# Quarter sums of normed x2 and the weight rests in a fast-multiplied MLP: from GpSimd to VectorE, with copies out of PSUM

## The chip, the cores and the metric

The kernel runs on one core of a Trainium2 chip. The metric is the device time of an execution in microseconds, the median over runs. TensorE does the matrix products, ScalarE and VectorE do elementwise work and may read PSUM, GpSimd works on SBUF alone and also issues the transfers that add to what lies in SBUF, SyncE issues the plain transfers.

## The reference

One layer of a hybrid decoder: x is normed and projected, three token mixers run side by side, their merged output is projected and added to x. The sum is called x2 here. Then comes the part that the change touches:

```python
h2 = rms_norm(x, norm_ffn[l])                       # x is x2 in the kernel; 512 tokens x 1024 channels
up = causal_dwconv(h2 @ w_up[l], ffn_conv_w[l], ffn_conv_b[l])   # w_up: 1024 x 6144
gate_h, val_h = jnp.split(up, 2, axis=-1)
x = x + (jax.nn.gelu(gate_h, approximate=True) * val_h) @ w_down[l]
return rms_norm(x, final_norm)
```

All values are float32.

## The kernel before

**Split products.** TensorE multiplies in a format with fewer bits than float32. So every operand is split in two: `hi` is a copy by ScalarE into that format (line 97), `lo` is what is left, source minus `hi`, by VectorE (line 98, called the rest below). `mm3` (line 104) adds up three products, hi x hi, hi x lo, lo x hi; the products with a weight's `lo` come last. `split(hi, lo, src, eng)` puts the rest on another engine if one is given.

**Order of the work.** The program is a list of units (the matmuls of one weight piece) and steps. Each unit carries preparations that are emitted a given number of units ahead: `load` (a plain transfer by SyncE), `add` (a transfer by GpSimd that adds a second piece of the weights to what was loaded), `ready` (the split). The framework then orders each engine's instructions at build time by priority in program order and by its own estimate of when they are ready; each engine runs its list strictly in order. Tiles of SBUF that come from `fslot` and `rslot` share 51 slots of 128 x 512 float32, given out in the order of the program. `sbank` has three PSUM banks (`sm` in the trace), `bank` five (`mm`).

**Norm of x2.** While the last part of the output projection runs, each of four token tiles t is normed (`norm2`, with the reciprocal root as a chain of tiny VectorE steps, lines 112 to 118) and transposed by TensorE, four 128 x 128 blocks to a bank (`norm2_flip`, line 1147). Each bank is split into `h2["h"]` and `h2["l"]`, which hold all 1024 channels by 512 tokens. Tiles 2 and 3 are transposed among the first units of the up projection.

**The up projection** has 24 gate and 24 value tiles of 128 channels. Eighteen pairs go the ordinary way (`up_units`: 24 matmuls of 128 x 512 each). Six pairs (numbers 3, 4, 6, 7, 9, 10) go a fast way (`up_fast`): a 2 x 2 block product with seven products in place of eight. The blocks on the token side are the quarters A11, A12, A21, A22 of normed x2 (first index: half of the tokens, second: half of the channels). Their sums are S1 = A21 - A22, S2 = S1 - A11, A11 - A21 and A12 + S2. On the weights' side the sums B11 + B12 and so on are made by the adding transfers, in the one buffer B11: for a1 as loaded, then plus B12 for c1, plus B22 for b1, plus B21 for b3. The seven parts are named a1, a2, c1, c2, b1, b2, b3; each is 12 matmuls of 128 x 256.

`h2_sums(p)` (p is one of two halves of the channels within a quarter) makes the sums on GpSimd: four additions hi + lo to get the quarters back, four sums (lines 1212 to 1217). `h2_ready(key, p)` splits one sum. `up_fast` runs the rests of a2, c2 and b2 on GpSimd, those of a1, c1, b1, b3 on VectorE.

Around the first fast pair the order is: units 0 to 2, `h2_sums(0)`, unit 3, `h2_sums(1)`, units 4 and 5, `h2_ready` of all four sums for p = 0, a1, unit 6, `h2_ready` of all four for p = 1, c1, a2, c2. Its b1, b2 and b3 run among the parts of the next fast pair, which begins with b1 of the pair ahead and then its own a1.

After the up tiles the down projection follows, fast for the first 20 of 24 channel tiles, with adding transfers of its own on GpSimd (line 299).

Of the kernel before, what the change touches and what calls it, by code (L numbers as in the profile page):

```python
# [8 lines left out]
F32 = mybir.dt.float32  # L9
# [4 lines left out]
AF = mybir.ActivationFunctionType  # L14
ALU = mybir.AluOpType
# [3 lines left out]
P = 128  # L19
# [23 lines left out]
HT = S // 2  # L43
# [14 lines left out]
def trunk(ctx: ExitStack, tc: tile.TileContext, x, xT, mem, memT, par, wdecay, wch, wv, wg, wmk,  # L58
          wmv, wrg, wbr, wout, wup, wdown, wdown2, gffn, gfin, out):
    nc = tc.nc  # L60
# [11 lines left out]
    def nm(s):  # L72
        uid[0] += 1
        return f"{s}_{uid[0]}"

    def fslot(shape=(P, S)):
        return apool.tile(list(shape), F32, tag="s", name=nm("f"))

    def rslot(shape=(P, S)):
        return apool.tile(list(shape), F32R, tag="s", name=nm("r"))  # L80
# [14 lines left out]
    def split(hi, lo, src, eng=None):  # L95

        nc.scalar.activation(hi, src, AF.Copy)  # L97
        return (eng or nc.vector).tensor_tensor(out=lo, in0=src, in1=hi.bitcast(F32), op=ALU.subtract)  # L98
# [34 lines left out]
    def unit(dram, n, fn, parts=1):  # L133

        w = {}
        i = sum(1 for k, *_ in prog if k == "unit")

        def ready():
            w["w"] = fetch(dram, n, parts)
            for h in behind.get(i, ()):  # L140
                h()
        prog.append(("unit", [(AHEAD, ready)], lambda: fn(w["w"])))

    def made_unit(pre, fn):

        prog.append(("unit", pre, fn))

    def step(fn):
        prog.append(("step", [], fn))
# [194 lines left out]
    def run(*parts):  # L344

        for p in parts:
            if isinstance(p, tuple):
                unit(*p)
            else:
                for v in p:  # L350
                    made_unit(*v) if isinstance(v, tuple) else step(v)
# [37 lines left out]
    def x_norm(k):  # L389

        f = xs["h", k] = fslot()
        nc.vector.scalar_tensor_tensor(out=f, in0=xs["T"][k], scalar=col(C_GMIX + k), in1=xs["rb"],  # L392
                                       op0=ALU.mult, op1=ALU.mult)
        split(hh[:, k, :], hl[:, k, :], f)
# [49 lines left out]
    xn = [lambda k=k: x_norm(k) for k in range(KD)]  # L444
# [198 lines left out]
    def branch(n, acts, d, gt=None):  # L643

        g = [gt]

        def gate(ps):
            g[0] = fslot()
            nc.scalar.activation(g[0], ps, AF.Sigmoid)

        def proj(w):
            pp = channel_major(w, NM, lambda k: acts[k])
            if n == BRANCHES[0]:
                merged.append(mslot())
                nc.vector.tensor_tensor(out=merged[d], in0=pp, in1=g[0], op=ALU.mult)
                return
            nc.vector.tensor_tensor(out=g[0], in0=pp, in1=g[0], op=ALU.mult)
            nc.vector.tensor_tensor(out=merged[d], in0=merged[d], in1=g[0], op=ALU.add)
            if n == BRANCHES[2]:
                r = (rslot(), rslot())  # L660
                split(*r, merged[d])
                mr.append(r)
        return [proj_in(18 + 8 * n + d, gate), (wbr[n, d], MIX, proj)]
# [103 lines left out]
    b2 = [u for d in range(KD) for u in branch(2, oc, d)]  # L767
# [173 lines left out]
    at = lambda a, i: by_chunk(a)[:, :, i:i + 1].broadcast_to([DK, NT, P])  # L941
# [188 lines left out]
                                       op0=ALU.mult, op1=ALU.mult)  # L1130
        return xn

    h2 = {}

    def norm2(t):
        y = rstd(t)
# [2 lines left out]
    def norm2_flip(t):  # L1139
        if t == 0:  # L1140
            h2["h"] = hpool.tile([P, KD, S], F32R, name="h2h", tag="hh")
            h2["l"] = hpool.tile([P, KD, S], F32R, name="h2l", tag="hl")
        xn = h2.pop(("xn", t))
        for g in range(2):
            pt = sbank((P, 4, P))
            for k in range(4):
                nc.tensor.transpose(pt[:, k, :], xn[g][:, k * P:(k + 1) * P], ident)
            split(*(h2[a][:, 4 * g:4 * g + 4, t * P:(t + 1) * P] for a in "hl"), pt)

    step(lambda: gain_rows(gffn))  # L1150
    wo = down_units(wout, lambda k: mr[k], norm2, norm2_flip)
# [52 lines left out]
    h2s = {}  # L1204

    def h2_sums(p):
        tt, f = nc.gpsimd.tensor_tensor, {}
        for r in range(2):
            for c in range(2):
                at = slice(4 * c + 2 * p, 4 * c + 2 * p + 2), slice(r * HT, (r + 1) * HT)  # L1210
                f[r, c] = fslot((P, 2, HT))
                tt(out=f[r, c], in0=h2["h"][(slice(None), *at)].bitcast(F32), in1=h2["l"][(slice(None), *at)].bitcast(F32),
                   op=ALU.add)
        tt(out=f[1, 1], in0=f[1, 0], in1=f[1, 1], op=ALU.subtract)
        tt(out=f[1, 0], in0=f[0, 0], in1=f[1, 0], op=ALU.subtract)
        tt(out=f[0, 0], in0=f[1, 1], in1=f[0, 0], op=ALU.subtract)
        tt(out=f[0, 1], in0=f[0, 1], in1=f[0, 0], op=ALU.add)
        h2s.update({("c1", p): f[1, 1], ("b2", p): f[1, 0], ("b1", p): f[0, 0], ("c2", p): f[0, 1]})

    def h2_ready(key, p):  # L1220
        f, h2s[key, p] = h2s[key, p], (rslot((P, 2, HT)), rslot((P, 2, HT)))
        split(*h2s[key, p], f)

# [6 lines left out]
    def up_fast(i, keep):  # L1230

        src = lambda q: wup[NF * (int(q[2]) - 1) + i][:, HB * (int(q[1]) - 1):HB * int(q[1])]
        raw, w, st = {}, {}, {}

        def load(q):
            raw[q] = fslot()
            loads.append(nc.sync.dma_start(raw[q], src(q)))

        def ready(key, q, more=None):
            w[key] = rslot(), rslot()  # L1240
            split(*w[key], raw[q], nc.gpsimd if key in ("a2", "c2", "b2") else None)
            if more:
                add(q, more)

        def add(q, more):
            nc.gpsimd.dma_start(raw[q], src(more), accum_op=ALU.add)

        def run(key):
            if key == "a1":
                st["x"], st["o"] = bank((P, HT)), (fslot(), fslot())  # L1250
            elif key in ("a2", "c1"):
                st[key] = sbank((P, HT))
            ps = st["c1" if key[0] == "c" else "a2" if key == "a2" else "x"]
            hi, lo = w.pop(key)
            k = range(KD // 2)
            mm3(ps, [(*(a[:, j * P:(j + 1) * P] for a in (hi, lo)), *h2_part(key, j)) for j in k],
                key in ("a1", "a2", "c1"), True, key not in ("a1", "a2", "c1"))
            (g, v), tt = st["o"], nc.vector.tensor_tensor

            one, two = slice(0, HT), slice(HT, S)  # L1260
            if key in ("a1", "c1", "c2", "b3"):
                o = {"a1": g[:, one], "c1": v[:, two], "c2": v[:, one], "b3": g[:, two]}[key]
                nc.scalar.activation(o, ps, AF.Copy)
            elif key == "a2":
                tt(out=g[:, one], in0=g[:, one], in1=ps, op=ALU.add)
            else:
                o = v[:, one if key == "b1" else two]
                tt(out=o, in0=o, in1=ps, op=ALU.subtract)
            if key == "b3":
                up_mix(*(up_evac(a, NF * half + i) for half, a in enumerate((g, v))), i, keep)  # L1270

        pre = {
            "a1": [(8, lambda: load("B11")), (3, lambda: ready("a1", "B11", "B12"))],
            "a2": [(6, lambda: load("B21")), (3, lambda: ready("a2", "B21"))],
            "c1": [(2, lambda: ready("c1", "B11", "B22"))],
            "c2": [(6, lambda: load("B22")), (3, lambda: ready("c2", "B22"))],
            "b1": [(2, lambda: ready("b1", "B11", "B21"))],
            "b2": [(9, lambda: load("B12")), (6, lambda: add("B12", "B22")), (3, lambda: ready("b2", "B12"))],
            "b3": [(2, lambda: ready("b3", "B11"))],
        }  # L1280
        return {key: (p, lambda key=key: run(key)) for key, p in pre.items()}
# [110 lines left out]
    def halves(i, a):  # L1392
# [2 lines left out]

    group = lambda first: lambda k: acts[first + k]
    us = up_units((0, 1, 2, 5, 8, 11), whole, 3)
    run(*us[:3], [lambda: h2_sums(0)], us[3], [lambda: h2_sums(1)], us[4], us[5],
        [lambda k=k: h2_ready(k, 0) for k in ("c1", "c2", "b1", "b2")])

    ahead = None
    for i, u in zip((3, 4, 6, 7, 9, 10), us[6:]):
        f = up_fast(i, whole)
        run([ahead["b1"]] if ahead else [], [f["a1"]], u)
        if not ahead:
            run([lambda k=k: h2_ready(k, 1) for k in ("c1", "c2", "b1", "b2")])
        run([ahead["b2"]] if ahead else [], [f["c1"], f["a2"]], [ahead["b3"]] if ahead else [], [f["c2"]])
        ahead = f
    us = up_units(range(12, 20), whole)
    run([ahead["b1"]], us[0], [ahead["b2"]], us[1], [ahead["b3"]])  # L1410
# [97 lines left out]
```

## Time and profile before

| | before |
|---|---|
| median of 3 runs | 935.45 us (934.63 to 937.51) |
| profiled execution | 935.83 us |
| its span, first to last instruction | 934.1 us |
| TensorE busy | 916.4 us (98%) |
| VectorE, ScalarE, GpSimd busy | 660.1, 518.3, 174.3 us |

The profile is of one execution. Times in it count from the start of the span. A row of a timeline gives start, duration, engine, line, operation, the tiles out<-in and the number merged into the row; in brackets stands the idle time ahead and what ended it. PE is TensorE's matmul, PEld its weight load, DVE VectorE, ACT ScalarE, POOL GpSimd, SP SyncE. A row of a group gives busy time and mean nanoseconds of one. The granted clock is the share of full speed that TensorE was given. In the trace, `r` is any split tile from `rslot`, `f` any tile from `fslot`, `wlo`/`whi` the split of an ordinary weight, `h2h`/`h2l` the split of normed x2.

### The profile page before, as it was taken

Reading aid. Unit: us, or ns where it says so; the run is one execution under the profiler, and the core shown is the slowest. Engines: PE = TensorE matmul, PEld = TensorE weight load, DVE = VectorE, ACT = ScalarE, POOL = GpSimd, SP = SyncE. Lnnn points to the kernel's source line nnn. Section 1 sums busy time; section 2 is a strip of 40 time slices with the busy share of each in tenths; the row PEclk is TensorE's granted clock in tenths of the full one; section 3 lists DMA queues with packets and bytes.
Section 4 is the critical chain, followed back from the end, with each engine's and each line's share of the span. In section 5 each row is a group of like instructions: output and inputs, shape, how many; then the busy total and the mean of one; then the engine's idle time right before and its main releaser. Section 6 shows DMA issues by size and latency. Waiting matters only on the chain.

```text
span 934.1 us, 12758 instructions
## 1 busy us (share of the span) xinstructions
PE 916.4 (98%) x4606; PEld 785.9 (84%) x4606; DVE 660.1 (71%) x1142; ACT 518.3 (55%) x872; POOL 174.3 (19%) x202
## 2 busy tenths in 40 slices
PE   9999999999999999999999999899999999999997
PEld 7898888888889998888888897899977888888885
DVE  6997754665788666847676758666787766688865
ACT  7675655684865577484434335455555445544544
POOL 0010000000233430330000136445410231013102
PEclk9999999999999999999999999899999999999999
DMA  7446223223369873321167214675645676356622
GB/s 255 135 136 207 95 78 100 87 74 117 99 145 207 188 196 107 116 77 46 57 184 254 69 35 125 150 177 128 144 113 158 135 210 150 95 136 183 150 68 90
DMA packets 51184, 123.28 MB, mean 132 GB/s; under 512 B 6145, under 2 KB 14001, under 8 KB 51121
## 3 DMA queue, kind: packets, MB, share of 16 engines
q1 hardware_dynamic: 35648, 94.99, 31.0%
q0 software_dynamic: 15328, 27.21, 16.9%
q8 instruction: 36, 0.59, 0.3%
q14 instruction: 28, 0.22, 0.1%
q10 hardware_dynamic: 144, 0.26, 0.1%
HBM read 117.99 MB, written 3.67 MB: 130 GB/s over the span
## 4 chain that ended last, share of the span: by engine, by line
PE 79%; DVE 9%; DMA 5%; issue 3%; ACT 2%; POOL 0%; SPq 0%; POOLq 0%; ACTq 0%; DVEq 0%
PE mm L104 71%; DMA f<-in_wup 3%; PE sm L104 3%; DVE wlo L98 2%; PE mm L436 2%; DVE r L98 2%; DMA raw<-in_wup 2%; DVE f L1164 1%; DMA f<-in_wdown 1%; ACT r L97 1%; ACT whi L97 0%; DVE f L1129 0%; PE sm L211 0%; DVE f L392 0%; PE sm L996 0%
## 5 line engine op out<-in xcount | busy, mean ns | idle before, releaser
L98 DVE TENSOR_TENSOR wlo<-raw,whi 128x1024 fp32r<-128x1024 f32 (+3 forms) x142 | 163.6, 1156 | 86.7 <-ACT whi L97 42.6
L97 ACT ACTIVATE whi<-raw 128x1024 fp32r<-128x1024 f32 (+3 forms) x142 | 135.6, 960 | 138.7 <-PE mm L104 107.4
L104 PE MATMUL mm<-whi,r 128*128 128x512 f32 (+2 forms) x568 | 171.9, 373 | 1.9 <-DVE r L98 1.9
L104 PEld LDWEIGHTS mm<-whi,r 128*128 128x128 f32 x568 | 105.4, 188 | 19.1 <-DVE r L98 3.5
L104 PE MATMUL mm<-hh,whi 128*128 128x512 f32 x288 | 113.3, 394 | 0.0
L104 PE MATMUL mm<-hl,whi 128*128 128x512 f32 x288 | 112.7, 391 | 0.0
L104 PE MATMUL mm<-wlo,r 128*128 128x512 f32 (+2 forms) x284 | 105.7, 372 | 0.5 <-DVE wlo L98 0.5
L104 PE MATMUL mm<-h2l,whi 128*128 128x512 f32 x264 | 102.8, 390 | 0.0
L104 PE MATMUL mm<-h2h,whi 128*128 128x512 f32 x264 | 102.7, 390 | 0.0
L104 PE MATMUL mm<-r,whi 128*128 128x512 f32 (+1 forms) x432 | 94.2, 367 | 0.0
L98 DVE TENSOR_TENSOR wlo<-f,whi 128x512 fp32r<-128x512 f32 (+2 forms) x90 | 53.7, 631 | 49.9 <-ACT whi L97 43.8
L98 DVE TENSOR_TENSOR r<-f,r 128x512 fp32r<-128x512 f32 (+3 forms) x126 | 73.0, 601 | 20.4 <-ACT r L97 20.0
L97 ACT ACTIVATE r<-f 128x512 fp32r<-128x512 f32 (+3 forms) x144 | 70.1, 534 | 30.1 <-DMA f<-in_wup 25.5
L104 PEld LDWEIGHTS mm<-r,whi 128*128 128x128 f32 x432 | 75.2, 189 | 13.1
L97 ACT ACTIVATE whi<-f 128x512 fp32r<-128x512 f32 (+2 forms) x90 | 48.1, 579 | 65.1 <-PE mm L104 47.3
L104 PE MATMUL mm<-hh,wlo 128*128 128x512 f32 x288 | 71.5, 390 | 0.0
L104 PE MATMUL mm<-r,r 128*128 128x512 f32 (+2 forms) x336 | 65.5, 346 | 0.0
L299 POOL DMA_DIRECT2D f<-in_wdown x40 | 35.1, 1041 | 162.2 <-DVE wlo L98 117.0
L104 PE MATMUL mm<-h2h,wlo 128*128 128x512 f32 x264 | 65.2, 389 | 0.0
L104 PEld LDWEIGHTS mm<-hh,wlo 128*128 128x128 f32 x288 | 54.0, 188 | 11.2
L104 PEld LDWEIGHTS mm<-hh,whi 128*128 128x128 f32 x288 | 54.1, 188 | 10.8
L104 PEld LDWEIGHTS mm<-hl,whi 128*128 128x128 f32 x288 | 54.1, 188 | 10.7
(262 smaller groups left out, 1613.1 us busy)
## 6 DMA issues: line engine op xcount, KB each, us to landing
raw<-in_wch SPq DMA_DIRECT2D x39, 512.0 KB, 3.4
raw<-in_wup SPq DMA_DIRECT2D x36, 512.0 KB, 4.0
f<-in_wdown POOLq DMA_DIRECT2D x40, 256.0 KB, 7.6
raw<-in_wbr SPq DMA_DIRECT2D x24, 384.0 KB, 3.1
raw<-in_wdown SPq DMA_DIRECT2D x14, 512.0 KB, 4.1
f<-in_wup SPq DMA_DIRECT2D x24, 256.0 KB, 6.8
f<-in_wup POOLq DMA_DIRECT2D x24, 256.0 KB, 5.7
f<-in_wdown SPq DMA_DIRECT2D x20, 256.0 KB, 5.7
```

The source lines that it names most:

```text
L97: nc.scalar.activation(hi, src, AF.Copy)
L98: return (eng or nc.vector).tensor_tensor(out=lo, in0=src, in1=hi.bitcast(F32), op=ALU.subtract)
L104: nc.tensor.matmul(ps, lhsT=l, rhs=r, start=first and i == 0, stop=last and i == len(seq) - 1, skip_group_check=more)
L299: nc.gpsimd.dma_start(raw[to, p][j], src(q, p)[:, j, :], accum_op=ALU.add)
L436: nc.tensor.matmul(ps[u], lhsT=w(a, u, k), rhs=xs["r"][k][j], start=k == 0 and i < n, stop=k == KD - 1 and i >= len(seq) - n)
L1164: nc.vector.scalar_tensor_tensor(out=a[:, j:], in0=ps[:, :S - j], scalar=col(C_FCW + 48 * (2 - j) + f), in1=a[:, j:], op0=ALU.mult, op1=AL ...
```

## The change

Five edits:

- `norm2_flip` copies each transposed bank out of PSUM by ScalarE, in two pieces of 128 x 256, into eight tiles that hold the quarters of normed x2 unsplit.
- `h2_sums` takes these quarters and makes three sums a half, on VectorE and in place; the fourth (A11 - A21) is made by `h2_sum3` when it is split.
- In `up_fast` the rests of a2, c2 and b2 go to VectorE.
- `h2_ready` moves: c1 for both halves ahead of unit 5, c2 behind unit 5, b1 and b2 behind c2 of the first fast pair.
- No arithmetic is left on GpSimd in the up projection; its adding transfers stay.

```diff
@@ norm2_flip
-        xn = h2.pop(("xn", t))
+        xn, pts = h2.pop(("xn", t)), []
         for g in range(2):
             pt = sbank((P, 4, P))
             for k in range(4):
                 nc.tensor.transpose(pt[:, k, :], xn[g][:, k * P:(k + 1) * P], ident)
             split(*(h2[a][:, 4 * g:4 * g + 4, t * P:(t + 1) * P] for a in "hl"), pt)
+            pts.append(pt)
+
+        for g, pt in enumerate(pts):
+            for p in range(2):
+                if t % 2 == 0:
+                    h2f[t // 2, g, p] = fslot((P, 2, HT))
+                nc.scalar.activation(h2f[t // 2, g, p][:, :, t % 2 * P:(t % 2 + 1) * P], pt[:, 2 * p:2 * p + 2, :], AF.Copy)
@@ h2_sums
-        tt, f = nc.gpsimd.tensor_tensor, {}
-        for r in range(2):
-            for c in range(2):
-                at = slice(4 * c + 2 * p, 4 * c + 2 * p + 2), slice(r * HT, (r + 1) * HT)
-                f[r, c] = fslot((P, 2, HT))
-                tt(out=f[r, c], in0=h2["h"][(slice(None), *at)].bitcast(F32), in1=h2["l"][(slice(None), *at)].bitcast(F32),
-                   op=ALU.add)
-        tt(out=f[1, 1], in0=f[1, 0], in1=f[1, 1], op=ALU.subtract)
-        tt(out=f[1, 0], in0=f[0, 0], in1=f[1, 0], op=ALU.subtract)
-        tt(out=f[0, 0], in0=f[1, 1], in1=f[0, 0], op=ALU.subtract)
-        tt(out=f[0, 1], in0=f[0, 1], in1=f[0, 0], op=ALU.add)
-        h2s.update({("c1", p): f[1, 1], ("b2", p): f[1, 0], ("b1", p): f[0, 0], ("c2", p): f[0, 1]})
+        sub, add = ALU.subtract, ALU.add
+        a11, a12, a21, a22 = (h2f.pop((r, c, p)) for r in range(2) for c in range(2))
+        s2 = fslot((P, 2, HT))
+        tt = nc.vector.tensor_tensor
+        tt(out=a22, in0=a21, in1=a22, op=sub)
+        tt(out=s2, in0=a22, in1=a11, op=sub)
+        tt(out=a12, in0=a12, in1=s2, op=add)
+        h2s.update({("c1", p): a22, ("c2", p): a12, ("b1", p): s2, ("b2", p): (a11, a21)})
+
+    def h2_sum3(p):
+        a11, a21 = h2s["b2", p]
+        nc.vector.tensor_tensor(out=a11, in0=a11, in1=a21, op=ALU.subtract)
+        h2s["b2", p] = a11
 
     def h2_ready(key, p):
+        if key == "b2":
+            h2_sum3(p)
         f, h2s[key, p] = h2s[key, p], (rslot((P, 2, HT)), rslot((P, 2, HT)))
         split(*h2s[key, p], f)
@@ up_fast, ready
-            split(*w[key], raw[q], nc.gpsimd if key in ("a2", "c2", "b2") else None)
+            split(*w[key], raw[q])
@@ the order around the first fast pair
-    run(*us[:3], [lambda: h2_sums(0)], us[3], [lambda: h2_sums(1)], us[4], us[5],
-        [lambda k=k: h2_ready(k, 0) for k in ("c1", "c2", "b1", "b2")])
+    run(*us[:3], [lambda: h2_sums(0)], us[3], [lambda: h2_sums(1)], us[4], [lambda: h2_ready("c1", 0), lambda: h2_ready("c1", 1)],
+        us[5], [lambda: h2_ready("c2", 0), lambda: h2_ready("c2", 1)])
...
         run([ahead["b1"]] if ahead else [], [f["a1"]], u)
+        run([ahead["b2"]] if ahead else [], [f["c1"], f["a2"]], [ahead["b3"]] if ahead else [], [f["c2"]])
         if not ahead:
-            run([lambda k=k: h2_ready(k, 1) for k in ("c1", "c2", "b1", "b2")])
-        run([ahead["b2"]] if ahead else [], [f["c1"], f["a2"]], [ahead["b3"]] if ahead else [], [f["c2"]])
+            run([lambda k=k, p=p: h2_ready(k, p) for k in ("b1", "b2") for p in range(2)])
```

2 lines of the change are left out of this document (1 added, 1 removed).

## The prediction

> **What bounds the kernel now.** I read the page's head, then TensorE's waits, then the stretches of the MLP (window table), then the timelines of the stretch that stands out. The head says how little there is to win: TensorE is busy in all but 17.7 us of the span, so a change to other engines can give back only its gaps and what a gap costs afterwards.
>
> ```profile
> span 934.1 us, 12758 instructions
> PE 916.4 (98%) x4606; PEld 785.9 (84%) x4606; DVE 660.1 (71%) x1142; ACT 518.3 (55%) x872; POOL 174.3 (19%) x202
> ```
>
> Two lines of TensorE's waits in the window 500 to 720 (what waits, for what: us in total, times, longest) and two of the window table (PE, PEld, DVE, ACT, POOL busy, then the granted clock):
>
> ```profile
> PE mm L104 <- DVE r L98: 3.2, 8, 1.0
> PE sm L104 <- POOL r L98: 2.7, 1, 2.7
> ...
> 580.20:586.30 6.10, 2.68 (x18) 2.19 (x17) 6.10 (x8) 4.44 (x8) 2.93 (x3) 1.00 0.35 93
> 586.30:593.10 6.80, 5.41 (x25) 4.97 (x24) 5.09 (x8) 3.47 (x7) 2.36 (x4) 0.50 0.69 245
> ```
>
> One hole carries most of it: from 580.2 to 586.3 TensorE works 2.68 of 6.10 us, and in the 6.8 us behind it the granted clock is 0.50. That is where the first fast tile runs its parts c1, a2, c2, b1:
>
> ```profile
> 580.21 0.73 PE L104 MATMUL sm<-r,r 128*128 128x256 f32 x4
> 581.68 0.39 PE L104 MATMUL sm<-h2h,r 128*128 128x256 f32 x1 [0.73 <-ACT r L97]
> ...
> 585.57 0.74 PE L104 MATMUL sm<-h2h,r 128*128 128x256 f32 x4 [2.69 <-POOL r L98]
> ...
> 587.36 1.86 PE L104 MATMUL sm<-r,r 128*128 128x256 f32 x7 [0.92 <-DVE r L98]
> 589.69 2.93 PE L104 MATMUL sm<-r,r 128*128 128x256 f32 x12 [0.47 <-ACT f L1263]
> ...
> 594.17 0.28 PE L104 MATMUL mm<-h2h,r 128*128 128x256 f32 x1
> ...
> 633.59 1.60 PE L104 MATMUL sm<-r,r 128*128 128x256 f32 x12
> 635.03 0.28 PE L104 MATMUL sm<-h2h,r 128*128 128x256 f32 x1
> ```
>
> A part of 12 matmuls takes 635.03 - 633.59 = 1.44 us when nothing waits, four take 5.8. Here they take 594.17 - 580.21 = 13.96. The hole costs 8.2 us: four waits of 0.73, 2.69, 0.92 and 0.47 (4.8 together), and some 3.4 from half speed (half of 6.8).
>
> Why it is there: GpSimd sums normed x2's quarters just ahead of it, and VectorE stands still meanwhile.
>
> ```profile
> 562.05 5.33 POOL L1212 TENSOR_TENSOR f<-h2h,h2l 128x512 f32<-128x512 f32 x4
> ...
> 562.84 5.64 DVE L98 TENSOR_TENSOR wlo<-raw,whi 128x1024 fp32r<-128x1024 f32 x1 [1.72 <-ACT whi L97]
> 569.95 1.59 DVE L1177 TENSOR_TENSOR f<-f,f 128x512 f32<-128x512 f32 x1
> 571.47 2.30 DVE L98 TENSOR_TENSOR wlo<-raw,whi 128x1024 fp32r<-128x1024 f32 x1
> 576.92 1.23 DVE L98 TENSOR_TENSOR wlo<-raw,whi 128x1024 fp32r<-128x1024 f32 x1 [1.71 <-ACT whi L97]
> 584.79 2.52 DVE L98 TENSOR_TENSOR r<-f,r 128x512 fp32r<-128x512 f32 x1
> ```
>
> The same 128x1024 rest takes 1.23 us with GpSimd quiet, 5.64 and 2.30 under its sums. With 0.68 for a 128x512 one (next fence), the excess is 4.41 + 0.91 + 1.07 + 1.84 = 8.2 us, on a queue that has one idle piece (1.71) from 562.84 until past 589.
>
> **The change part by part.** Rows that price it: two groups of GpSimd over the run, three of VectorE in the window 545 to 711, one of ScalarE.
>
> ```profile
> L98 POOL TENSOR_TENSOR r<-f,r 128x512 fp32r<-128x512 f32 x18 | 26.5, 1482 | 29.3 <-ACT r L97 27.6 <-DMA f<-in_wup 1.1 <-DVE f L1164 0.6
> L1212 POOL TENSOR_TENSOR f<-h2h,h2l 128x512 f32<-128x512 f32 x8 | 10.4, 1446 | 129.5 <-DVE st L116 117.2 <-DVE h2l L98 12.3
> ...
> L98 DVE TENSOR_TENSOR r<-f,r 128x512 fp32r<-128x512 f32 x32 | 26.2, 838 | 18.6 <-ACT r L97 18.5
> L98 DVE TENSOR_TENSOR wlo<-raw,whi 128x1024 fp32r<-128x1024 f32 x12 | 20.8, 1737 | 8.9 <-ACT whi L97 4.9 <-PE mm L104 4.0
> L98 DVE TENSOR_TENSOR h2l<-sm,h2h 128x512 fp32r<-128x512 f32 x3 | 2.0, 684 | 1.9 <-ACT h2h L97 1.9
> ...
> L1263 ACT ACTIVATE f<-sm 128x256 f32<-128x256 f32 x12 | 4.4, 370 | 3.4 <-PE sm L104 3.4
> ```
>
> *VectorE's bill.* It gets 18 rests (three for each of six fast tiles) and 8 quarter sums (six in h2_sums, two in h2_sum3), 26 x 0.684 = 17.8 us. It gets back what GpSimd took: 32 x (0.838 - 0.684) = 4.9 on rests and 12 x (1.737 - 1.23) = 6.1 on weight rests, 11 at least. So its busy time grows by about 7 us over 165, nothing where it idles; what counts is the place. GpSimd's 18 rests and 16 sums go to nothing.
>
> *Copies on ScalarE.* Sixteen of 128x256 from PSUM, 16 x 0.37 = 5.9 us, twelve of them in a stretch where ScalarE is busy 6.84 of 27 us, the last four behind the transposes at 546.86, where only the sums wait for them.
>
> ```profile
> 520.00:547.00 27.00, 26.23 (x162) 23.23 (x161) 21.43 (x72) 6.84 (x16) 2.55 (x2) 1.00 0.09 26
> ...
> 544.94 0.68 DVE L98 TENSOR_TENSOR h2l<-sm,h2h 128x512 fp32r<-128x512 f32 x1
> ...
> 546.86 1.04 PE L1147 MATMUL sm<-ident,f 128*128 128x128 f32 x8
> ```
>
> A copy reads the bank that VectorE's rest reads. If it must wait for that rest, the last copies of token tile 2 run from 545.6 to 546.4, and the transposes of tile 3, which want the bank, begin at 546.86: hidden by 0.4 us. Below zero is excluded; above, two copies late would cost 0.7. I take 0. What is queued behind a waiting copy on ScalarE is only the next tile's high parts, 1.5 us away in the same rows. [...]
>
> *Ahead of the hole.* GpSimd's first two sums stretch two of VectorE's one-column reciprocal-root steps, 0.16 us each when undisturbed, to 0.81 and 1.22: 1.7 us in the chain that ends in the rests TensorE waits for at 545.
>
> ```profile
> 534.04 2.55 POOL L1212 TENSOR_TENSOR f<-h2h,h2l 128x512 f32<-128x512 f32 x2 [117.23 <-DVE st L116]
> ...
> 534.54 0.81 DVE L117 TENSOR_TENSOR st<-st,st 128x1 f32<-128x1 f32 x1
> 535.39 1.22 DVE L118 SCALAR_TENSOR_TENSOR st<-st,st 128x1 f32<-128x1 f32 x1
> 536.64 0.16 DVE L116 TENSOR_TENSOR st<-st 128x1 f32<-128x1 f32 x1
> ...
> 545.08 0.74 PE L104 MATMUL mm<-h2h,r 128*128 128x256 f32 x4 [0.31 <-DVE r L98]
> ...
> 546.28 0.74 PE L104 MATMUL mm<-h2h,r 128*128 128x256 f32 x4 [0.46 <-DVE r L98]
> ```
>
> Both waits are shorter than 1.7, so -0.8 (bounds: 0, should the order change, and -0.8).
>
> *The hole itself.* VectorE had split c1's weights at about 583.1, just before the transfer in the next fence could be issued. From 562.84 to there are 20.2 us; less 1.71 idle and the first three excesses (4.41, 0.91, 1.07) that is 12.1 us of unstretched work. Afterwards it has three to six quarter sums more (2.1 to 4.1), the two rests of c1's second half now ahead of c1's weights (1.4), less the two of b1 and b2 now behind (1.4). That ends c1's weight rest near 578 to 579 instead of 583, before TensorE wants it (580.2, its last four matmuls 1 us later). a2's rest follows at +0.7, c2's at +1.4 or with a weight rest between at +2.5, against needs of 582.6 and 584. So c1, a2 and c2 run without a wait: end 580.2 + 4.3 = 584.5. Next late is b1. Its weights are B11 plus a transfer that GpSimd may issue only when c1's split has read B11:
>
> ```profile
> 583.37 0.86 POOL L1246 DMA_DIRECT2D f<-in_wup  x1 [7.62 <-DVE r L98]
> ...
> f<-in_wup POOLq DMA_DIRECT2D x24, 256.0 KB, 5.7
> ```
>
> Issued near 578.5, landed at 584.2 to 585, split on ScalarE and VectorE by 586; and b1's own quarter sums are split behind it, because slots are given out in program order and h2_ready("b1") now stands after c2. Four more splits in a row, 0.6 each: b1 ends near 588.2 and the next a1 near 589.6, not at 587.4. I take 2.2 us lost here (bounds 0.5 and 3.6, by the landing). Gain 8.2 - 2.2 = 6.0, if the clock stays up.
>
> *The later fast tiles.* b3's rest is late by a quarter us in two tiles, because GpSimd does a rest before it issues the transfer that b3 reads:
>
> ```profile
> 637.92 0.74 PE L104 MATMUL mm<-h2h,r 128*128 128x256 f32 x4 [0.25 <-DVE r L98]
> ...
> 632.35 0.69 DVE L98 TENSOR_TENSOR r<-f,r 128x512 fp32r<-128x512 f32 x1 [3.81 <-ACT r L97]
> ...
> 634.21 1.77 POOL L1246 DMA_DIRECT2D f<-in_wup  x2
> ```
>
> VectorE ended at 633.04, the issue came at 634.21. With no rest on GpSimd it comes 1.1 us sooner: -0.5 for both. VectorE's three extra rests a tile (2.05) lie in its idle pieces, such as the 3.81. If that cover were gone, the whole 2.05 would show, six times 2.05 = 12.3.
>
> *Not touched.* Of the 3.2 us, what is left (about 1.9) are four waits from 694 to 708 for the down projection's activations. Nothing of the change stands in their chain, so I leave them.
>
> Sum: -6.0 - 0.8 - 0.5 = -7.3 on a profiled execution of 935.83 us (span 934.1 and 1.7 around it). That execution lies 0.4 above the median of 935.45, so I forecast 928.1 for the median.
>
> **The rivals.** *The clock falls again.* It fell with 3.4 us of idle time inside 6.1. If b1's wait comes to about that, half speed costs up to 3.4 once more: near 931.5. For it: the wait I expect (2.2) is of that kind. Against: it is a third less, and comes behind full work. [...]
>
> *The change doesn't do what it says.* Up to c1's split VectorE is given six sums (4.1) and two rests (1.4) for the 8.2 it gets back. If GpSimd's sums are only half of what stretches it (transfers write to SBUF at the same time), 4.1 comes back for 5.5 and the hole stays: 934 to 937. Against: the 5.64 begins and ends with the 5.33 of GpSimd's row, and the next rest but one, with transfers running, takes 1.23.
>
> *Slower: VectorE sets the pace of the fast tiles.* The mechanism is one: c1's weights are split only 0.55 us before TensorE takes them (633.04 against 633.59), and need to be complete 0.96 later. A rest put into VectorE's queue ahead of that one, and itself waiting for a transfer, holds it. From 1.5 us of delay a tile TensorE pays. To eat 7.3 us it must pay 1.2 us in each of six tiles; were all 2.05 us paid, 928.1 + 12.3 = 940.4.
>
> **How the numbers follow.** Likeliest as summed, 0.50: 925.6 (nothing lost at b1: 935.45 - 9.5 = 925.9, rounded down) to 930. Below that, with part of the 1.9 gone as well, 0.05. Clock falls again, 0.22: 930 to 933. No gain, 0.13: 933 to 938. Slower, 0.10: 938 to 941. A difference below 0.3% (2.8 us) is about what a measurement of this kernel can't tell from no change: faster means below 932.6, slower above 938.3. Faster 0.50 + 0.05 + 0.21 = 0.76, within 0.14, slower 0.10. The range leaves out the slow case and the two tails: 924.5 to 935.5.
>
> **What would show it.** Right: no GpSimd rows but transfers from 520 to 680; VectorE's 128x1024 rests at 1.23 throughout; c1, a2 and c2 in the first fast tile in 4.3 us with clock 1.00; a short wait at b1 with ScalarE held by a transfer. Wrong at its root: VectorE rests still stretched with GpSimd quiet; the same 2.69 under another releaser; or waits for VectorE's r of more than 1 us in every fast tile.

## The result and the profile after

| | before | after |
|---|---|---|
| median of 4 runs | 935.88 us | 923.61 us (922.28 to 924.37) |
| ratio, 95% interval | 1 | 0.9866 (0.9846 to 0.9886) |
| the same kernels again, with the experiments | 935.98 us | 924.64 us, ratio 0.9873 (0.9855 to 0.9892) |
| profiled execution, its span | 935.83, 934.1 us | 924.37, 922.6 us |

The kernel is about 12 us faster, 3.5 to 4.5 more than by the forecast of 928.1, and its first median lies just under the range (924.5 to 935.5). The page's head and, from it, TensorE's waits between 500 and 720 us after the change:

```profile
span 922.6 us, 12732 instructions
PE 912.0 (99%) x4606; PEld 784.1 (85%) x4606; DVE 657.2 (71%) x1168; ACT 524.1 (57%) x888; POOL 128.1 (14%) x168
```

```profile
PE mm L104 <- DVE f L1278: 0.7, 1, 0.7
PE mm L104 <- ACT r L97: 0.3, 1, 0.3
PE mm L104 <- ACT h2h L97: 0.2, 1, 0.2
```

None of the eight waits for VectorE's `r` (3.2 us) and not the one for GpSimd's (2.7) is left in this profile; one new wait is there, 0.68 us for VectorE to read a PSUM bank. (A second profile of the same kernel, a_again below, has two waits for VectorE's `r` again, 0.8 us together, and not the new one.) TensorE's row of the window from unit 6 to unit 7, where the hole was (PE, PEld, DVE, ACT, POOL busy, granted clock, DMA share, GB/s), and its timeline there:

```profile
577.27:590.57 13.30, 13.04 (x85) 11.81 (x84) 9.13 (x15) 7.16 (x13) 2.58 (x3) 1.00 0.75 191
```

```profile
577.27 1.98 PE L104 MATMUL mm<-h2h,wlo 128*128 128x512 f32 x8
579.09 1.60 PE L104 MATMUL sm<-r,r 128*128 128x256 f32 x12
...
581.96 1.60 PE L104 MATMUL sm<-r,r 128*128 128x256 f32 x12
...
584.05 0.39 PE L104 MATMUL mm<-r,r 128*128 128x256 f32 x1 [0.26 <-ACT r L97]
...
585.84 1.00 PE L104 MATMUL mm<-r,r 128*128 128x256 f32 x7
586.68 0.40 PE L104 MATMUL mm<-h2h,r 128*128 128x256 f32 x2
```

c1, a2 and c2 follow each other without a pause from 579.09 to 583.40. Then the matmuls of b1 (`r,r`) and of the next a1 (`h2h,r`) alternate, and one wait of 0.26 is all that is left. VectorE just ahead of it, with no arithmetic on GpSimd:

```profile
570.07 0.68 DVE L98 TENSOR_TENSOR r<-f,r 128x512 fp32r<-128x512 f32 x1
572.44 1.23 DVE L98 TENSOR_TENSOR wlo<-raw,whi 128x1024 fp32r<-128x1024 f32 x1 [1.70 <-ACT whi L97]
```

**Where the time came from.** I cut the region into three stages at TensorE's first matmuls with a weight's rest (`h2h,wlo`) of one unit: from the first transpose of normed x2 to unit 6; from unit 6 to unit 7 (the hole); from unit 7 to a unit in the middle of the down projection's first stretch. The two last bounds in the kernel before and the kernel after:

```profile
578.32 0.84 PE L104 MATMUL mm<-h2h,wlo 128*128 128x512 f32 x3
599.27 1.07 PE L104 MATMUL mm<-h2h,wlo 128*128 128x512 f32 x4
...
713.02 1.30 PE L104 MATMUL mm<-h2h,wlo 128*128 128x512 f32 x5
```

```profile
577.27 1.07 PE L104 MATMUL mm<-h2h,wlo 128*128 128x512 f32 x4
590.57 0.61 PE L104 MATMUL mm<-h2h,wlo 128*128 128x512 f32 x2
...
701.43 0.84 PE L104 MATMUL mm<-h2h,wlo 128*128 128x512 f32 x3
```

All kernels in one table, each stage from one profile (both profiles where there are two), in us. Each ratio is to the kernel before as timed together with that kernel (its medians there are 935.88 to 936.84), so kernels are better compared by ratio than by median:

| kernel | to unit 6 | the hole | unit 7 to 713 | sum | median | ratio (95%) |
|---|---|---|---|---|---|---|
| before | 53.55, 53.41 | 20.95, 20.46 | 113.75, 114.30 | 188.2 | 936 | 1 |
| after | 52.39, 52.26 | 13.30, 13.20 | 110.86, 111.62 | 176.8 | 923.61, 924.64 | 0.9866, 0.9873 |
| b_rests | 53.61 | 20.89 | 109.13 | 183.6 | 932.96 | 0.9966 (0.9955 to 0.9978) |
| b_order | 53.22 | 18.68 | 113.03 | 184.9 | 935.05 | 0.9984 (0.9970 to 0.9999) |
| a_oldorder | 52.56 | 18.90 | 109.12 | 180.6 | 928.50 | 0.9914 (0.9899 to 0.9930) |
| a_gprests | 52.57 | 14.18 | 114.54 | 181.3 | 928.73 | 0.9923 (0.9908 to 0.9939) |
| a_dummy | 54.13 | 19.43 | 109.27 | 182.8 | 930.93 | 0.9940 (0.9925 to 0.9954) |
| a_b12early | 52.58 | 13.67 | 112.40 | 178.7 | 926.12 | 0.9887 (0.9867 to 0.9906) |
| a_nocopies | 52.26 | 16.70 | 111.35 | 180.3 | 928.42 | 0.9908 (0.9890 to 0.9926) |
| a_lastb2 | 52.27 | 13.40 | 110.83 | 176.5 | 925.39 | 0.9879 (0.9859 to 0.9899) |
| a_zrests | 52.26 | 14.73 | 114.71 | 181.7 | 931.10 | 0.9943 (0.9929 to 0.9956) |
| a_b1first | 52.28 | 14.24 | 109.13 | 175.7 | 925.26 | 0.9880 (0.9863 to 0.9897) |
| b_load7 | 54.16 | 21.37 | 112.12 | 187.7 | 937.23 | 1.0009 (0.9996 to 1.0022) |
| a_load7 | 52.57 | 13.15 | 109.71 | 175.4 | 924.27 | 0.9878 (0.9855 to 0.9901) |
| b_lastb2 | 53.96 | 21.31 | 112.29 | 187.6 | 935.27 | 0.9993 (0.9980 to 1.0006) |

So the change gave 1.2 us up to unit 6, 7.5 in the hole and 2.8 behind it, together 11.4 of the 11.3 to 12.3 by the medians. Among kernels that do the same there, the first two columns spread by up to 0.9 us. The third spreads by 1.5 where GpSimd makes all 18 rests (113.0 to 114.5 in before, b_order and a_gprests) and by 3.3 where it makes none (109.1 to 112.4 in the kernel after, b_rests, a_oldorder, a_dummy, a_b12early, a_nocopies and a_b1first). The two groups don't overlap, but differences within a group are not read from one profile. The expectations split the third column once more, at the low-part matmuls of 690.91 (682.36 after): "later fast tiles" are 91.64 us before and 91.79 after, the "first down-projection stage" 22.11 and 19.07.

### The profile page after: what moved, and what is told of

It reads as the page before. It is cut to its first block, busy times and chain, and to the rows that moved or that the text cites. A ratio compares the mean times of both kernels' runs of the same rounds, so it can differ in the third digit from the quotient of the medians.

```text
span 922.6 us, 12732 instructions
## 1 busy us (share of the span) xinstructions
PE 912.0 (99%) x4606; PEld 784.1 (85%) x4606; DVE 657.2 (71%) x1168; ACT 524.1 (57%) x888; POOL 128.1 (14%) x168
## 4 chain that ended last, share of the span: by engine, by line
PE 87%; DMA 5%; DVE 3%; issue 2%; ACT 2%; POOL 0%; SPq 0%; DVEq 0%; POOLq 0%; ACTq 0%
PE mm L104 78%; DMA f<-in_wup 4%; PE sm L104 3%; DMA f<-in_wv 2%; PE mm L436 2%; DVE wlo L98 1%; DVE r L98 1%; ACT r L97 1%; PE sm L211 0%; PE sm L996 0%; PE sm L983 0%; PE sm L1010 0%; DVE f L810 0%; PE sm L1147 0%; PE sm L601 0%
## 5 line engine op out<-in xcount | busy, mean ns | idle before, releaser
L98 DVE TENSOR_TENSOR wlo<-raw,whi 128x1024 fp32r<-128x1024 f32 (+3 forms) x142 | 157.4, 1113 | 82.8 <-ACT whi L97 39.4
L98 DVE TENSOR_TENSOR r<-f,r 128x512 fp32r<-128x512 f32 (+3 forms) x144 | 79.7, 577 | 23.0 <-ACT r L97 22.7
L104 PEld LDWEIGHTS mm<-r,r 128*128 128x128 f32 (+1 forms) x336 | 53.3, 186 | 9.6 <-ACT r L97 0.5
```

Source lines behind the costliest of these rows:

```text
L104: nc.tensor.matmul(ps, lhsT=l, rhs=r, start=first and i == 0, stop=last and i == len(seq) - 1, skip_group_check=more)
```

## The experiments

**The rests alone.** b_rests: the line of `ready` as in the kernel after, all else as before.

```diff
-            split(*w[key], raw[q], nc.gpsimd if key in ("a2", "c2", "b2") else None)
+            split(*w[key], raw[q])
```

> The kernel before, with one part of the change alone: the rests of the weight sums of a2, c2 and b2 on VectorE; the sums of the quarters stay on GpSimd and the order of their splits is the old one. Theory A (GpSimd's sums stretch VectorE and so make the hole): the 128x1024 rests of 5.6 and 2.3 us stay, c1, a2, c2 and b1 of the first fast tile still need 12 to 15 us, b3's small waits go (-0.5), and the time is 935 down to 932, the lower end if GpSimd's last rest was also what made the down projection 3 us late. Theory C (a2's rest on GpSimd is the cause, the 2.69 us wait): the hole shrinks by that wait and by the half clock behind it, some 6 us, to 928 to 930.

932.96 us, so 3.2 us gained by the ratio, none of it in the hole (20.89): there the rest that TensorE waits for is merely made by another engine. The 2.69 us for GpSimd's `r` turn into waits for VectorE's:

```profile
585.44 0.73 PE L104 MATMUL sm<-h2h,r 128*128 128x256 f32 x4 [1.97 <-DVE r L98]
586.01 0.28 PE L104 MATMUL sm<-r,r 128*128 128x256 f32 x1
587.95 1.86 PE L104 MATMUL sm<-r,r 128*128 128x256 f32 x7 [1.66 <-DVE r L98]
```

Theory C falls. The gain is all behind unit 7: 109.13 for 114, which is 4.9 us in a profile that ran 1.2 us under this kernel's median. The change as a whole shows only 2.8 there. The three kernels with no rests on GpSimd but a hole of 18.9 us or more (b_rests, a_oldorder, a_dummy) have 109.1 to 109.3, so part of what the closed hole saves may be waited for again behind it; a_b1first has 109.13 with the hole closed, so this is not shown.

**The rests back.** a_gprests: the kernel after with that line as before.

> The kernel after, with the rests of a2, c2 and b2 back on GpSimd; the sums stay on VectorE from ScalarE's copies, in the new order. Theory A: the hole stays closed (c1 and a2 without a wait over 1 us); b3's quarter-us waits come back. If the 3.0 us of the first down-projection stage hang on the rest on GpSimd ahead of it, they are lost too: 926 to 927.5; if they hang on something else, 924 to 925. Theory C: a wait for GpSimd's rest of 2 us or more in the first fast tile and 929 or more.

928.73 us. The hole stays closed (14.18), no wait for GpSimd's `r` comes back, and the third column is as long as before (114.54). That is theory A, but with 1.2 us more than its upper end; the 0.5 us that I gave for the rests can no longer be right.

**The old order.** a_oldorder: the kernel after, `h2_ready` called where it was.

```diff
-    us[4], [lambda: h2_ready("c1", 0), lambda: h2_ready("c1", 1)],
-        us[5], [lambda: h2_ready("c2", 0), lambda: h2_ready("c2", 1)])
+    us[4], us[5],
+        [lambda k=k: h2_ready(k, 0) for k in ("c1", "c2", "b1", "b2")])
...
+            run([lambda k=k: h2_ready(k, 1) for k in ("c1", "c2", "b1", "b2")])
```

> The kernel after, with the order of the quarters' splits put back (all four of the first half behind the sixth unit, all four of the second ahead of c1); sums and rests stay on VectorE. Theory A: VectorE has four rests (2.7 us) more ahead of c1's weights, which were ready about 1.7 us early: a wait of 0.5 to 2 us at c1 or a2, clock 1.00, 924 to 927. Theory B (the order is what fills the hole): most of 7.6 us comes back, 929 to 932.

928.50. No arithmetic on GpSimd, and the hole is there all the same: 18.90.

```profile
582.27 0.74 PE L104 MATMUL sm<-h2h,r 128*128 128x256 f32 x4 [0.55 <-DVE r L98]
...
584.79 1.60 PE L104 MATMUL sm<-r,r 128*128 128x256 f32 x7 [1.66 <-DVE r L98]
586.96 2.93 PE L104 MATMUL sm<-r,r 128*128 128x256 f32 x12 [0.57 <-ACT f L1273]
```

```profile
585.20:592.00 6.80, 6.22 (x29) 5.93 (x29) 3.98 (x7) 3.36 (x7) 1.75 (x2) 0.50 0.70 197
```

Each wait is as short as I expected (0.55, 1.66, 0.57), but I had written "clock 1.00": 6.8 us at half clock come on top, by estimate 3.4 us lost. So the price is near theory B's, by a mechanism that neither theory had in its number.

**The order alone.** b_order: the kernel before with the new calls of `h2_ready`, nothing else.

> The kernel before, with the new order of the quarters' splits alone; sums and rests stay on GpSimd. From the four runs so far the stage from u6 to u7 (the first fast tile's hole) took 20.9 us in the kernel before, 18.9 with the sums moved but the old order, 13.3 in the kernel after, and 19.4 with the dummy sums in the new order. Theory AB (the hole closes only when both go, GpSimd's sums and the four rests ahead of c1's weights): 18.5 to 20.5 us here, the later fast tiles 1 to 2 us longer, the time 934 to 937. Theory B (the order does it by itself, the dummy sums spoilt it in another way): 13 to 15 us, 928 to 930.

935.05, the hole 18.68. Theory AB holds: each half of the cure alone takes about 2 of the 7.5 us, both together all of it. Here a wait of 2.67 us for c1's weights is left, two short ones (0.35, 0.54) at the next a1 and b1, and 3.4 us at half clock.

**The sums' work without the sums.** a_dummy: in `h2_sums` of the kernel after,

```diff
+        z, g = fslot((P, 2, HT)), nc.gpsimd.tensor_tensor
...
+                g(out=z, in0=h2["h"][(slice(None), *at)].bitcast(F32), in1=h2["l"][(slice(None), *at)].bitcast(F32), op=add)
+        for op in (sub, sub, sub, add):
+            g(out=z, in0=z, in1=z, op=op)
```

> The kernel after, with GpSimd's sixteen sums added back at their old place, from the same operands but into a scratch slot that nobody reads. Theory A: VectorE's rests are stretched again where GpSimd's sums run (128x1024 rests of over 4 us), c1's weights are late, and at least half of the 7.6 us comes back: 928 to 932, with a stretch of lower clock in the first fast tile. Rival (it is the place of the sums in VectorE's own chain, or the new order, not the stretch): 923 to 925.

930.93, with 1.8 us lost ahead of unit 6 as well. GpSimd, then VectorE beside it, in that kernel:

```profile
565.82 7.27 POOL L1221 TENSOR_TENSOR f<-h2h,h2l 128x512 f32<-128x512 f32 x4
573.17 6.25 POOL L1223 TENSOR_TENSOR f<-f 128x512 f32<-128x512 f32 x4
```

```profile
565.54 3.00 DVE L98 TENSOR_TENSOR wlo<-raw,whi 128x1024 fp32r<-128x1024 f32 x1
568.46 0.74 DVE L1171 SCALAR_TENSOR_TENSOR f<-mm,prm,f 128x511 f32<-128x511 f32 x1
569.12 1.12 DVE L1226 TENSOR_TENSOR f<-f,f 128x512 f32<-128x512 f32 x1
...
571.87 1.78 DVE L1184 TENSOR_TENSOR f<-f,f 128x512 f32<-128x512 f32 x1
...
575.01 2.06 DVE L98 TENSOR_TENSOR wlo<-raw,whi 128x1024 fp32r<-128x1024 f32 x1
```

Nobody waits for these sums, and VectorE's rests of 1.23 us take 3.00 and 2.06: the stretch is shown. (I expected one of over 4.) The scratch also holds slots out of the 51; what that does by itself was not tried.

**Which part of the order.** a_b12early: b1's and b2's splits alone back at their old places, for p = 0 behind c2's and ahead of a1, for p = 1 ahead of c1.

```diff
+        [lambda k=k: h2_ready(k, 0) for k in ("b1", "b2")])
...
+            run([lambda k=k: h2_ready(k, 1) for k in ("b1", "b2")])
```

> The kernel after, with the splits of b1's and b2's quarters alone put back to their old places, ahead of c1's weights; those of c1 and c2 stay where the change put them. If the four rests of b1 and b2 ahead of c1's and a2's weights (4 x 0.68 = 2.7 us of VectorE) are what the old order cost: u6 to u7 17 to 19 us with a stretch of lower clock, later fast tiles 90.1 us again (1.7 less than after), 926 to 929. If it is c1's and c2's earlier place that matters: u6 to u7 13 to 14.5 us, 922 to 924.

The hole is 13.67: it is the early place of c1's and c2's splits that matters, for both halves, not that b1's and b2's come later. I had expected the reverse as the first case. By time it is not told apart from the kernel after: 0.9887 against 0.9866 and 0.9873, with intervals that overlap.

**Without the copies.** a_nocopies: no copies by ScalarE, `h2_sums` as before but with `tt = nc.vector.tensor_tensor`.

> The kernel after, without ScalarE's sixteen copies out of PSUM: VectorE makes each quarter itself as high part plus rest, then the sums (16 operations instead of 8; 8 x 0.68 = 5.5 us more on VectorE between 534 and 575). If VectorE has room there: 923 to 925 and the copies buy nothing. If it has not, as in the old order, where 2.7 us of rests cost 5.6: c1's weights late, u6 to u7 16 to 19 us, 926 to 930.

928.42, the hole 16.70. VectorE has no room for eight more operations there; four waits of 0.38, 0.70, 0.17 and 1.61 us come back, this time at full clock. By the ratios the copies buy 3 to 4 us.

**One rest back.** a_lastb2, and its mirror in the kernel before, b_lastb2:

```diff
-            split(*w[key], raw[q])
+            split(*w[key], raw[q], nc.gpsimd if (key, i) == ("b2", 10) else None)
```

> The kernel after, with one single rest back on GpSimd: b2's of the last fast tile, the last instruction but the transfers that GpSimd had ahead of the down projection. Theory D (this rest made the first down-projection stage 3 us late: it stretches VectorE's gate products, the activation behind them and the split that releases the weights' transfers): the stage from the last gate unit to the third down unit takes 21 to 22 us instead of 19.1, VectorE's row of four gate products takes about 3.8 us instead of 2.7, the transfers land 6 us or more after their issue; 925.5 to 927. Rival (the earlier rests on GpSimd, or the order of the whole list): 19.1 us as before and 923.6 within 0.5.

> The kernel before, with one single rest moved to VectorE: b2's of the last fast tile. In the kernel after, the same rest put back cost 1.7 us in the first down-projection stage (20.8 for 19.1). If that rest is the cause here too: the stage takes 20 to 20.5 us instead of 22.1, 934 to 935. If the fast tiles ahead bring the lateness (their last b3 rest comes 5.9 us ahead of the last gate unit where TensorE waits for it, 6.5 to 8 where it doesn't, and the transfers follow from that): 21.5 to 22.1 us and no measurable difference.

(Times with a plus sign in these count from the low-part matmuls two units earlier, at 677.11 in the kernel before.) The stage took 20.77 us in a_lastb2, about what theory D wanted, but its fast tiles took 90.06, 1.7 less than in the kernel after, although both have the same lists up to the last of them; 925.39 can't be told from 924.64. b_lastb2: stage 20.85, between my two cases, and no measurable gain in time. So one rest is not seen to be the cause, and D stays unproven, because of the next run.

**The kernel after a second time.**

> The kernel after, unchanged, profiled a second time, to see which of its stages repeat. In the first profile two later fast tiles took 16.78 and 16.03 us instead of 15.54, though the kernel with one rest put back (the same lists of instructions up to its last fast tile) had 15.54 in all. If that is the spread of the transfers from one execution to the next: 90.1 us for the fast tiles here, the first down-projection stage 19.1 again, the span 920.5 to 921.5. If it belongs to the new order: 91.8 again.

90.44 us for the fast tiles as hoped, but 21.18, not 19.07, for the down-projection stage. So the 3 us that the first pair of profiles showed at 690 to 712 are not a property of the change: the same program has them in one execution and not in the other. What differs between the profiles is how late weights come. The rows below show GpSimd's adding transfer ahead of the request, SP's request, and ScalarE's split of the weights that SP asked for: in the kernel before, in the kernel after, and in the second profile of the latter.

```profile
678.92 1.76 POOL L299 DMA_DIRECT2D f<-in_wdown  x2 [3.28 <-DVE wlo L98]
...
680.87 2.37 SPq L294 DMA_DIRECT2D f<-in_wdown  x4
...
688.35 1.25 ACT L97 ACTIVATE whi<-f 128x512 fp32r<-128x512 f32 x2 [5.29 <-DMA f<-in_wdown]
```

```profile
668.94 0.87 POOL L299 DMA_DIRECT2D f<-in_wdown  x1 [5.05 <-PE mm L104]
...
672.32 1.81 SPq L294 DMA_DIRECT2D f<-in_wdown  x4
...
676.67 1.25 ACT L97 ACTIVATE whi<-f 128x512 fp32r<-128x512 f32 x2 [2.16 <-DMA f<-in_wdown]
```

```profile
668.02 0.87 POOL L299 DMA_DIRECT2D f<-in_wdown  x1 [4.71 <-issue]
...
670.41 1.83 SPq L294 DMA_DIRECT2D f<-in_wdown  x4
...
677.00 1.24 ACT L97 ACTIVATE whi<-f 128x512 fp32r<-128x512 f32 x2 [4.38 <-PE mm L104]
```

From request to split: 7.5, 4.4 and 6.6 us, with the first adding transfer 1.95, 3.4 and 2.4 us ahead of the request. (The last row names TensorE; the transfer landed at 676.92, just before the split.) In these three profiles the split comes later the closer the adding transfer is ahead; it was not tested by itself.

**Asking earlier.** b_load7 and a_load7: `seven` gets a parameter for how far ahead a1's weights are asked for, 7 units instead of 6 in the first stretch; SP then has that request ahead of a 512 KB load.

> The kernel before, with one edit far from the change: the weights of the first down-projection stage's second a1 part are asked for one unit earlier, so that they stand ahead of a 512 KB load in SP's queue and not behind it. GpSimd's sums and rests stay. Theory D2 (the stage is late in the kernel before because these weights are asked for at +3.76 us after the last gate unit, just behind two accumulating transfers that GpSimd issued at +1.81, and land 7.4 us later): they now land before ScalarE wants them, the stage from the last gate unit to the third down unit takes 19 to 20 us instead of 22.1, 933 to 934.5. Rival (VectorE's backlog behind the stretched gate products sets it): 22 us as before, 936 or slower.

> The kernel after, with the same earlier request. Theory D2: the stage is already free of these waits, so nothing to gain there: 19.1 us and 923.6 within 0.7, or slightly faster in those executions in which the weights come late. If the earlier request takes a slot or bandwidth from the last fast tiles: waits there, 925 to 927.

D2's mechanism fits, and what I gave as its worth was wrong. In the kernel before the stage takes 19.13 us with GpSimd's rests all in place (22.11 and 21.43 without the edit), and the waits from 694 to 708 are gone. But the fast tiles take 92.99, and the last of them has TensorE wait 2.06 us: the adding transfer that it needs took 7.3 us to land beside the earlier request, against 4.9 in the first profile of the kernel before; the second has a wait of 0.83 at the same place and 92.87 for the fast tiles.

```profile
657.51 0.74 PE L104 MATMUL mm<-h2h,r 128*128 128x256 f32 x4 [0.26 <-DVE r L98]
677.28 1.70 PE L104 MATMUL mm<-r,r 128*128 128x256 f32 x12 [2.06 <-ACT r L97]
```

So lateness seems to move between the fast tiles and this stage, which is why only their sum is in the table. Of the 1.6 to 2.2 us that the sum still gains, the time shows nothing (937.23); the rest of that profile is longer in places that the edit leaves alone, and why was not found. a_load7 has the stage at 19.07 and is no faster than the kernel after, and no other version was.

**GpSimd's rests as mere work.** a_zrests: VectorE makes all rests that TensorE uses; beside those of a2, c2 and b2

```diff
+                nc.gpsimd.tensor_tensor(out=zz[0], in0=zz[1], in1=w[key][0].bitcast(F32), op=ALU.subtract)
```

> The kernel after, with eighteen subtractions put back on GpSimd where the rests of a2, c2 and b2 stood, of the same size, from the same high parts and at the same place in GpSimd's queue, but into a scratch tile that nobody reads; VectorE still makes the rests that TensorE uses. Theory S (GpSimd's work is what costs, by stretching VectorE and by standing ahead of the transfers): most of what the rests on GpSimd cost comes back (928.7 against 924): 927 to 930, VectorE's rests and gate products stretched beside it. Rival (TensorE waited for the slower engine's result itself): 923.5 to 925.

931.10: theory S, and above its 927 to 930. No operand comes from GpSimd, and more than a_gprests' loss is back. The stand-in is heavier than what it stands for: its eighteen subtractions take 1.74 us each, 31.3 together, against 1.45 and 26.1 for the rests in a_gprests, and VectorE makes its own eighteen rests beside them. So 7 us is not the price of the rests themselves; by a_gprests that is 4 to 5. VectorE's groups in the fast tiles (596 to 672 us), kernel after, then a_zrests:

```profile
L98 DVE TENSOR_TENSOR r<-f,r 128x512 fp32r<-128x512 f32 x32 | 21.1, 687 | 16.9 <-ACT r L97 16.9
...
L98 DVE TENSOR_TENSOR wlo<-raw,whi 128x1024 fp32r<-128x1024 f32 x4 | 4.9, 1225 | 2.8 <-PE mm L104 2.2 <-ACT whi L97 0.5
L1171 DVE SCALAR_TENSOR_TENSOR f<-mm,prm,f 128x511 f32<-128x511 f32 x5 | 3.7, 746 | 0.4 <-ACT f L1169 0.4
```

```profile
L98 DVE TENSOR_TENSOR r<-f,r 128x512 fp32r<-128x512 f32 x31 | 27.0, 898 | 11.5 <-ACT r L97 11.4
...
L98 DVE TENSOR_TENSOR wlo<-raw,whi 128x1024 fp32r<-128x1024 f32 x4 | 7.4, 1854 | 0.5 <-ACT whi L97 0.5
...
L1171 DVE SCALAR_TENSOR_TENSOR f<-mm,prm,f 128x511 f32<-128x511 f32 x5 | 3.7, 739 | 0.0
```

Rests grow from 687 to 898 ns and from 1225 to 1854. How much of the 7 us is this stretch and how much the adding transfers queued behind the work on GpSimd was not separated.

**b1 ahead of the next a1.** a_b1first: a1's matmuls are made to depend on b1's last one.

```diff
+            with tc.issue_after(b1last.pop()) if key == "a1" and b1last else ExitStack():
```

> The kernel after, with one dependency more: the matmuls of the second fast tile's a1 come behind the first tile's b1, in the order that the prediction assumed, and no longer between b1's. If the interleaving is what saved the 2.2 us predicted as lost at b1: a wait of 1 to 2 us at b1, u6 to u7 14.5 to 15.5 us instead of 13.3, 925 to 926. If b1's weights simply came earlier than predicted (their transfer landed 4.1 us after its issue, not 5.7): 13.2 to 13.8 us and no measurable difference.

Waits of 0.42 and 0.34 us at b1, the hole 14.24: 1.0 us longer than with the parts interleaved. In between: both reasons hold.

**The kernel before a second time.**

> The kernel before, unchanged, profiled a second time. If its stages repeat: 20.9 us from u6 to u7, 91.6 for the later fast tiles, 22.1 for the first down-projection stage. If the last two are as free as in the kernel after (91.8 and 19.1 in one execution, 90.4 and 21.2 in the other), their sum lies between 112 and 114.5 us all the same, 2 to 3 above that kernel's 110.9 and 111.6.

20.46 for the hole, 92.87 and 21.43 for the two stages behind, together 114.30. The 2.8 us between the kernels in the third column stand.

## Why the prediction was wrong in size and right in direction

- *Ahead of the hole, -0.8.* Measured -1.2; the waits of 0.31 and 0.46 us are gone. Right. b_order, with GpSimd's sums in place, keeps the time (53.22); a_oldorder, without them, has the gain.
- *The hole, -6.0.* Measured -7.5. The forecast for c1, a2 and c2 (4.3 us, clock 1.00, no wait) came out: 583.40 - 579.09 = 4.31. Over-sized was what I took as lost at b1, "2.2 us lost here": about 0.6 was lost. The transfer behind it went out at 577.69 (I had 578.5) and was split at 581.81, 4.1 us and not 5.7, and a1's matmuls fill b1's wait, worth 1.0 by a_b1first. My "b1 ... and the next a1" in this order was a reading of the program's order; the build-time order is another.
- *Why the hole was there.* I laid all 8.2 us on the stretch of VectorE and booked the order of the splits as nothing (1.4 ahead, 1.4 behind). The stretch is real (a_dummy), but taken away alone it gives 1.8 (a_oldorder, 20.7 to 18.9), and the order alone 2.0 (b_order). That the figure for the hole came out as near as it did, with this cause for it, is luck: the change has both. And it is c1's and c2's place that counts, not the "two of b1 and b2 now behind".
- *The later fast tiles, -0.5, and "Not touched ... Nothing of the change stands in their chain, so I leave them".* This is the step that failed. Behind unit 7 the change gives 2.8 us; the rests alone give 3.2 (ratio 0.9966). I saw GpSimd's rests as a delay of 1.1 us of one issue. They also stretch VectorE all through the fast tiles (its 128x512 rests take 848 ns between 596 and 672 us, 687 in the kernel after) and stand ahead of adding transfers (in the kernel before, the rest of 632.97 takes until 634.26, and the transfer behind it goes out at 634.21), and somewhat heavier subtractions, read by nobody, cost 7 us (a_zrests). The waits at 694 to 708 that I left alone hung on SP's request and the 7.5 us until its split; I did not follow them back past VectorE's `r`. With the request one unit earlier they are gone (b_load7), and with the rests on VectorE too (b_rests). That the lateness of the fast tiles is handed on there is read from the rows; the share of each link was not isolated.
- *Copies, 0.* That a copy waits for VectorE's rest of the same bank was an assumption of mine; no run of the kernel before shows it. In the profile of the kernel after, the copies from each bank do start behind that rest: the one of 543.76 ends at 544.45 and the copies from that bank run from 544.48 to 545.14, 0.67 us ahead of the transposes of tile 3 at 545.81. Why they wait is not shown. No cost shows in any stage; without them, and with VectorE making the quarters itself, 3 to 4 us are lost.
- *VectorE's bill, +7.* Measured -2.9 (660.1 to 657.2). 26 operations of 0.684 us were added, so 20.7 us came back, not 11: the products of gate and value (994 ns in the kernel before between 596 and 672 us, 685 after) and the convolution's 128x510 steps on SBUF (875 and 745) had been stretched too. It did not enter the sum.
- *The rivals.* The clock did not fall in the kernel after (1.00 from 500 to 720 us), though with the old order or the dummy sums it did (0.50 for 6.8 and 3.4 us). The wait for VectorE of 0.68 us in one later tile of one profile is the rival "VectorE sets the pace" at about a twentieth of its price. The change does what it says.

The case "with part of the 1.9 gone as well" had a chance of 0.05; it is about what happened.

## What to carry to other kernels

Arithmetic on GpSimd beside a busy VectorE was paid here in VectorE's own time (rests of 848 ns for 687), and it held back transfers queued behind it (in the kernel before one went out at 634.21, 1.2 us after VectorE's end at 633.04; what that costs alone was not separated); price it by stretched rows of the whole stage, not by the one wait that names GpSimd. When a change moves work and its place in the order, try both alone before giving either the credit: here each was worth 2 us in the hole, together 7.5. And profile the same kernel twice before reading a stage's 2 or 3 us as an effect: a transfer that lands late in one execution may not in the next (in the kernel after, 4.4 us from request to split in one profile and 6.6 in the other).

## What the runs showed of the hardware

**The stretch is selective.** VectorE's operations with two operands in SBUF grow beside GpSimd's arithmetic (687 to 898 ns, 1225 to 1854), the ones that read PSUM and one SBUF tile don't (746 and 739 ns in the two groups above; 0.74 us at 568.46 in a_dummy). These means mix operations that met GpSimd with ones that didn't, and some that were under way when GpSimd's began kept their time (743 ns at 609.67 in the kernel before). One at a time it is sharper; VectorE, then GpSimd, in the kernel before:

```profile
619.10 0.74 DVE L1164 SCALAR_TENSOR_TENSOR f<-mm,prm,f 128x510 f32<-128x510 f32 x1
619.76 0.95 DVE L98 TENSOR_TENSOR r<-f,r 128x512 fp32r<-128x512 f32 x1
```

```profile
618.78 1.37 POOL L98 TENSOR_TENSOR r<-f,r 128x512 fp32r<-128x512 f32 x1
```

The step that reads PSUM runs its 0.74 us inside GpSimd's rest. VectorE's rest ends at 620.71, 0.56 after GpSimd's end at 620.15. So it is with all twelve operations that were stretched by more than 0.12 us between 600 and 676 there: they end 0.55 to 0.56 us after GpSimd's (128x512 and 128x510) or 1.09 (128x1024), whether GpSimd's had 0.4 or 2.1 us to go. That looks like standing still until GpSimd is done, not like a slower pace; what would hold them is not shown.

**The clock fell behind short waits.** TensorE's longest wait in the first fast tile was 2.69 us (in the kernel before), and half clock came in pieces of 3.4 us (b_order, a_dummy) or 6.8 (before, b_rests, a_oldorder). In b_load7 it lasted longer by the rows: 12 matmuls from 593.32 take 2.72 us and the next 12 still 2.16, against 1.44 at full clock. Rows of the window table of b_order and of a_dummy, around the half-clock piece:

```profile
585.50:588.90 3.40, 3.40 (x18) 3.40 (x17) 1.11 (x2) 0.52 (x1) 1.06 (x1) 0.50 0.91 217
```

```profile
593.40:596.80 3.40, 3.40 (x18) 3.40 (x18) 1.94 (x4) 1.31 (x3) 0.21 (x1) 0.50 1.05 248
```

It came after 2.67 us in one wait (b_order), after 1.87 and 0.54 within 3 us (a_dummy), after 0.55 and 1.66 within 3.1 us (a_oldorder), and not after 1.61 alone (a_nocopies, clock 1.00 from 578 to 594) or 2.06 alone (b_load7, where the next 12 matmuls take 1.54 us). So 2.21 us of idle time in two waits were enough in one run, and 2.06 in one wait were not in another. These rows show no threshold, and whether it matters where a wait falls was not tested.
